# A list scheduler's cost model replaced, and the first loads of a two-layer encoder rearranged

## The chip, the cores and the metric

The kernel runs on one core of one Trainium2 chip. The time is device microseconds (us) of one launch, and the number that counts is the median over runs; before the change it is 1318.05 us (3 runs, 1318.02 to 1319.16).

## The reference

Two layers over 512 tokens of 1024 channels. Each layer modulates a normalised input, projects it, runs three token mixers beside each other, gates and merges them, and adds the result to the input:

```python
c_act = jax.nn.silu(c)
for l in range(DEPTH):
    mod = c_act @ w_ada[l] + b_ada[l]
    shift, scale, gate = jnp.split(mod, 3, axis=-1)
    h = rms_norm(x, norm_w[l]) * (1.0 + scale[:, None, :]) + shift[:, None, :]
    proj = h @ w_in[l]
    ya = mixer_a(...) * silu(ga)   # grouped-query attention, rotary
    yb = mixer_b(...) * silu(gb)   # banded dilated attention, relative bias
    yc = mixer_c(...)              # bidirectional state-space scan, its own gate
    merged = g_a * (ya @ w_proj_a[l]) + g_b * (yb @ w_proj_b[l]) + g_c * (yc @ w_proj_c[l])
    x = x + gate[:, None, :] * (merged @ w_out[l])
```

## The kernel before

Channels lie on partitions and tokens on the free axis. Weights come as chunks of 128x1024 float32 (512 KB; `wch`, 84 a layer). Each is split into a high part (ACT cast, `whi` or `u`) and a low part (a DVE subtraction, `wlo` or `u`), and each product of one 128-channel tile is three matmuls of 128x512: high x high, high x low, low x high (`mm_k`, L490). A whole chunk is 24 of them.

**Modulation.** A load of `w_ada` (128x1024, 512 KB, called an ada here) gives one column of `mod`. `ada` (L637) multiplies it by the broadcast activation `cbc` and sums along the row: on DVE as one instruction with an accumulator, or, for the shifts of tiles 0 to 6 of layer 0 (`POOLADA`, L413), as a GpSimd multiplication (engine POOL) and an ACT pass that sums. Tile i of the normalised input (`norm_tile`, L720) needs the scale `mod[i]` and the shift `mod[8+i]`: DVE makes `tmp`, ACT makes the high part `h`, DVE the low part `h`.

**The start.** `setup` (L534) loads c, the eight tiles of x (`merged<-in_xT`), the vector of small parameters, the identity and the tables of the relative bias, all on SP's queue. `record` (L1307) then goes over the eight tiles: two adas, up to three chunks at a time (`START_W`), the tile, and all matmuls of the `START` chunks (five) that it allows. Each of the five accumulates in a bank of its own. The three bias products (`bias_rows`, L602) come ahead of this.

**The planner.** All instructions are recorded first (`Rec.record`, L199), each with an estimated cost per engine (`cost_pe` to `cost_pool`, L132 to L167) and its predecessors. `Rec.schedule` (L277) is a list scheduler: it keeps an estimated clock, and hands each free engine the ready instruction of the lowest number, if storage can be had. Some instructions may run on one of two or three engines (`either`, L195; `any2`, `scale_p`, `sub`), and go to whichever the plan finds free first. The order found is fixed in the program: each engine works through its list in order. `issue` (L397) emits it, so nearly every instruction in the trace stands at L404.

**Mixer C.** For each of 8 heads and 4 blocks (`ssd_head`, L1162): a diagonal block scaled by a step (`bias<-const,dt`: ACT, POOL or DVE), two scans on DVE (`P<-ps_sc,bias`), an addition (`P<-P`), products with `cb` (`u<-P,u`), a cast on ACT (`u<-u`), the low part (`u<-u`, 128x1024, POOL or DVE), and matmuls into `ps_pv`. The convolution of the next tile (`conv`, L1093: `xs<-tmp,const,xs`, DVE) and fill work for PE (`pump`) lie in between.

Of the kernel before, what the change touches and what calls it, by code (L numbers as in the profile page):

```python
# [36 lines left out]
class V:  # L37
# [68 lines left out]

    def custom(self, fn):
# [16 lines left out]
class Op:  # L124
    __slots__ = ("i", "prio", "alts", "deps", "nd", "succ", "tiles", "frees", "start", "end", "eng", "dma", "ready", "urgent")


LAT = 200
# [3 lines left out]
def cost_pe(name, kw, args):  # L132
    if name == "transpose":
        return max(56, 0.417 * args[1].p * 2 + 2, 0.83 * args[1].n)
    l, r = kw["lhsT"], kw["rhs"]
    if r.dt == F32:
        return 2 * max(0.833 * r.n + 2, 0.833 * l.n, 25)
    return max(0.417 * r.n + 2.5, 0.833 * l.n, 25)


def cost_dve(name, out, ins, ptr, n):
    ps = any(v.t.psum for v in ins) or out.t.psum
    if name == "reciprocal":
        return 69 + 6.25 * n
    if name == "tensor_tensor_scan":
        return 69 + SCAN * n
    if name == "memset":
        return 40 + 0.5 * n
    two = len([v for v in ins if v.n and v.n > 1 and v.n >= n]) > 1
    if not two and not ps and name != "tensor_reduce":  # L150
        return 69 + 0.52 * n + 61 * ptr
    return 69 + 1.042 * n + 61 * ptr


def cost_act(name, out, ins, ptr, acc, n):
    return (52 if ins and ins[0].t.psum else 94) + 0.833 * n + 93 * bool(ptr) + 93 * acc


def cost_pool(name, out, ins, ptr, n):
    if name in ("tensor_scalar",):  # L160
        return 245 + 0.83 * n
    if name == "memset":
        return 100 + 0.4 * n
    return 148 + (2.1 if all(v.n == n and not v.wide for v in ins) else 1.67) * n
# [15 lines left out]
class Rec:  # L180
# [8 lines left out]
    margin = 200  # L189
    wait = 0.4  # L190
# [8 lines left out]
    def record(self, alts):  # L199
# [6 lines left out]
        for eng, meth, args, kw in alts:  # L206
# [11 lines left out]
            if meth == "dma_start":  # L218
                v = out if isinstance(out, V) else reads[0]
                op.dma = v.n * v.p * 4  # L220
                c = 520
            elif eng == "tensor":
                c = cost_pe(meth, kw, args)
            elif eng == "vector":
                if meth == "tensor_reduce":
                    n = reads[0].n
                c = cost_dve(meth, out, reads, ptr, n)
# [6 lines left out]
            op.alts[ENG[eng]] = (c, eng, meth, args, kw)  # L234
        deps = {}
        pe = eng == "tensor"
        for v in reads:
            for o, box, w in v.t.log:
                if w and self.meet(box, v.box):
                    deps[o] = LAT  # L240
        for v in writes:
            if pe and v.t.psum and v.t.lastpe is not None:
                deps.setdefault(v.t.lastpe, 0)
            for o, box, w in v.t.log:
                if o is not op and self.meet(box, v.box) and not (pe and "PE" in o.alts):
                    deps[o] = LAT
# [15 lines left out]
        if op.dma and self.hold is not None:  # L262
            op.alts = {e: (650,) + a[1:] for e, a in op.alts.items()}
# [13 lines left out]
    def schedule(self, reserve):  # L277
# [10 lines left out]
        dma_free, cold = 0.0, 0.0  # L288
        done, now, order = 0, 0.0, []
# [29 lines left out]
        while done < total:  # L319
# [6 lines left out]
            for e in ready:  # L326
                while free[e] <= now and ready[e]:
                    skipped, pick = [], None
                    while ready[e]:
                        it = heapq.heappop(ready[e])  # L330
                        o = it[2]
                        if o.i in started:
                            continue
                        if can_alloc(o, now) and not (soon and waits(o, e)):
                            pick = o
                            break
                        skipped.append(it)
                    for it in skipped:
# [17 lines left out]
                    if e == "PE":  # L356
                        if now - free[e] > 1500:
                            cold = now + 3400
                        if now < cold:
                            c *= 2  # L360
                    o.start, o.eng = now, e
                    free[e] = now + c
                    if o.dma:
                        s = max(now + 1300, dma_free)
                        dma_free = s + max(o.dma / 358.0, 60)
                        o.end = dma_free + 1000
                    else:
                        o.end = now + c
                    order.append(o)
                    done += 1  # L370
                    for z in o.tiles:
                        z.left -= 1
                        z.until = max(z.until, o.end)
                        if z.left == 0:
                            slots[z.tag].append((z.until + LAT, z.slot))
                    for q in o.succ:
                        q.ready = max(q.ready, o.end + q.deps[o] + (self.margin if "PE" in q.alts and e != "PE" else 0))
# [9 lines left out]
            nxt += [f for fr in slots.values() for f, _ in fr if f > now]  # L387
# [1124 lines left out]
```

## Time and profile before

| | us |
|---|---|
| median of 3 runs | 1318.05 |
| profiled execution | 1322.19 |
| its span, first to last instruction | 1320.4 |
| PE (TensorE) busy | 1234.5 |
| DVE (VectorE) busy | 1040.2 |
| ACT (ScalarE) busy | 667.4 |
| POOL (GpSimd) busy | 373.3 |

Busy counts an instruction from its start to its end, so an instruction that is held up within counts as busy for all of that time. A matmul row's length is longer than its share of PE, since matmuls are pipelined: the distance between the starts of two rows, divided by the count, is what one costs. The same goes for DVE.

### The profile page before, as it was taken

To read this page: it belongs to the slowest core of one execution; us is meant where nothing else is said; L and a number is where in the kernel's file an instruction comes from. 1 tells how busy PE (TensorE), PEld (TensorE's weight loads), DVE (VectorE), ACT (ScalarE), POOL (GpSimd) and SP (SyncE) were. 2 spreads that over 40 slices of the span, in tenths; PEclk is the share of its full clock that TensorE was granted. 3 is DMA by queue.
4 is the path that set the end of the run, shared out by engine and by line. 5 is a ranking of instruction groups with operands and counts; after the bars stand their busy time and mean duration, and the time that the engine had idled before them with its cause. 6 is when DMAs were issued, how large, how long until landed. Compare 5 with 4: busy or idle time off the path is not lost.

```text
span 1320.4 us, 17528 instructions
## 1 busy us (share of the span) xinstructions
PE 1234.5 (93%) x6240; PEld 1002.4 (76%) x6240; DVE 1040.2 (79%) x1798; ACT 667.4 (51%) x1132; POOL 373.3 (28%) x322
## 2 busy tenths in 40 slices
PE   4899999989999888999999999999998988989998
PEld 1678888778777667778888788887876866767887
DVE  7979975978799989974675999476598998998642
ACT  4447764666555445333334477556565443543330
POOL 3321220011035759610111222100002268583100
PEclk9999999999999999999999999999999999999999
DMA  7644214545322222234632421253342221222441
GB/s 283 237 122 121 69 47 154 187 140 178 108 59 78 64 64 64 66 110 144 222 129 63 130 96 50 79 183 89 95 132 56 81 64 55 73 64 80 136 137 63
DMA packets 49429, 144.30 MB, mean 109 GB/s; under 512 B 7350, under 2 KB 10038, under 8 KB 49342
## 3 DMA queue, kind: packets, MB, share of 16 engines
q1 hardware_dynamic: 49342, 143.19, 34.9%
q8 instruction: 49, 0.80, 0.3%
q14 instruction: 38, 0.31, 0.1%
HBM read 124.74 MB, written 4.27 MB: 98 GB/s over the span
## 4 chain that ended last, share of the span: by engine, by line
PE 63%; DVE 19%; POOL 7%; ACT 4%; issue 3%; DMA 3%; SPq 1%; DVEq 0%; POOLq 0%; ACTq 0%
PE ps_mm L404 47%; PE ps_sc L404 6%; PE ps_tp L404 6%; PE ps_pv L404 5%; DVE P L404 3%; DVE u L404 3%; POOL u L404 3%; DVE wlo L404 3%; DVE xs L404 2%; POOL P L404 1%; DVE q L404 1%; ACT u L404 1%; POOL bias L404 1%; DVE tmp L404 1%; ACT tmp L404 1%
## 5 line engine op out<-in xcount | busy, mean ns | idle before, releaser
L404 PE MATMUL ps_mm<-h,whi 128*128 128x512 f32 x1840 | 601.4, 397 | 1.8 <-ACT gate L404 1.5
L404 PEld LDWEIGHTS ps_mm<-h,whi 128*128 128x128 f32 x1840 | 345.3, 190 | 77.9 <-ACT gate L404 4.8
L404 PE MATMUL ps_mm<-h,wlo 128*128 128x512 f32 x920 | 364.6, 396 | 0.0
L404 DVE TENSOR_TENSOR wlo<-wraw,whi 128x1024 fp32r<-128x1024 f32 x158 | 208.4, 1321 | 84.6 <-ACT whi L404 83.2
L404 ACT CAST whi<-wraw 128x1024 fp32r<-128x1024 f32 x158 | 165.6, 1049 | 179.6 <-PE ps_mm L404 161.1
L404 PEld LDWEIGHTS ps_mm<-h,wlo 128*128 128x128 f32 x920 | 174.4, 190 | 34.7
L404 PE MATMUL ps_mm<-u,whi 128*128 128x512 f32 (+1 forms) x592 | 172.7, 374 | 0.0
L404 POOL TENSOR_SCALAR P<-P,s 128x512 f32<-128x512 f32 (+1 forms) x63 | 54.9, 873 | 339.3 <-DVE s L404 236.0
L404 PE MATMUL ps_pv<-u,u 128*128 128x256 f32 (+2 forms) x640 | 107.0, 293 | 28.4 <-ACT u L404 15.0
L404 PEld LDWEIGHTS ps_mm<-u,whi 128*128 128x128 f32 x592 | 107.7, 188 | 20.0 <-DVE gate L404 0.6
L404 PEld LDWEIGHTS ps_pv<-u,u 128*128 128x128 f32 (+1 forms) x640 | 81.3, 173 | 48.8 <-ACT u L404 21.2
L404 PE MATMUL ps_mm<-u,wlo 128*128 128x512 f32 (+1 forms) x296 | 110.0, 373 | 0.0
L404 ACT CAST u<-ps_tp 128x512 fp32r<-128x512 f32 (+2 forms) x174 | 71.8, 428 | 57.0 <-PE ps_tp L404 47.6
L404 DVE TENSOR_TENSOR_SCAN P<-ps_sc,bias 128x128 f32<-128x128 f32 (+3 forms) x128 | 98.7, 803 | 0.1
L404 DVE TENSOR_TENSOR u<-ps_tp,u 128x512 fp32r<-128x512 f32 (+2 forms) x174 | 81.9, 487 | 19.6 <-ACT u L404 18.9
L404 PE MATMUL ps_sc<-u,q 128*128 128x256 f32 (+1 forms) x320 | 85.9, 365 | 5.5 <-DMA u<-u 3.5
L404 POOL TENSOR_TENSOR tmp<-tmp,tmp 128x512 fp32r<-128x512 f32 (+1 forms) x22 | 32.4, 1474 | 180.4 <-ACT tmp L404 177.4
L404 POOL TENSOR_TENSOR u<-P,u 128x384 f32<-128x384 f32 (+3 forms) x68 | 69.3, 1030 | 15.0 <-DVE P L404 11.4
L404 PE MATMUL ps_tp<-const,P 128*128 128x128 f32 x448 | 67.6, 273 | 5.6 <-DVE s L404 2.3
L404 PEld LDWEIGHTS ps_tp<-const,P 128*128 128x128 f32 x448 | 53.7, 140 | 19.8 <-issue 7.2
L404 PEld LDWEIGHTS ps_sc<-u,q 128*128 128x128 f32 x320 | 52.9, 191 | 19.8 <-issue 6.5
L404 POOL TENSOR_TENSOR u<-u,u 128x1024 fp32r<-128x1024 f32 x24 | 62.3, 2595 | 12.8 <-ACT u L404 12.8
(163 smaller groups left out, 1892.0 us busy)
## 6 DMA issues: line engine op xcount, KB each, us to landing
wraw<-in_wch SPq DMA_DIRECT2D x168, 512.0 KB, 3.6
wraw<-in_wada SPq DMA_DIRECT2D x32, 512.0 KB, 3.8
u<-u SPq DMA_DIRECT2D x28, 256.0 KB, 3.2
merged<-in_xT SPq DMA_DIRECT2D x16, 256.0 KB, 3.2
whi<-in_wada SPq DMA_DIRECT2D x8, 512.0 KB, 4.9
wlo<-in_wada SPq DMA_DIRECT2D x8, 512.0 KB, 9.0
u<-u SPq DMA_DIRECT2D x64, 64.0 KB, 2.6
tmp<-xs SPq DMA_DIRECT2D x40, 64.0 KB, 2.1
```

Source lines behind the costliest of these rows:

```text
L404: getattr(getattr(nc, eng), meth)(*[get(a) for a in args], **{k: get(v) for k, v in kw.items()})
```

## The change

The planner's numbers are new. Each engine gets a cost and, apart from it, a time to the result (`DVE_TAIL` and the like) in place of one latency of 200; strided views cost more (`apart`); and an instruction that reads two SBUF operands on DVE, or any but memset on POOL, takes a common port, which the plan gives to one of the two at a time. Loads cost more on the queue, and a load between two places in SBUF counts twice its bytes. The planner's reserve for `ps_mm` and its `SOON` change too.

At the start no ada goes to POOL. The shifts of tiles 0, 1 and 2 (adas 8, 9, 10) come in another layout, and PE makes them with eight float32 matmuls of 128x1 each; the other 13 adas go to DVE. The parameters, the identity and a column form of c are loaded from POOL's queue. The bias tables and their products come after the early chunks, and these are six.

```diff
+DVE_TAIL, ACT_TAIL, POOL_TAIL, PE_TAIL = 115, 135, 120, 210
 def cost_dve(...):
-    two = len([v for v in ins if v.n and v.n > 1 and v.n >= n]) > 1
-    if not two and not ps and name != "tensor_reduce":
-        return 69 + 0.52 * n + 61 * ptr
-    return 69 + 1.042 * n + 61 * ptr
+    port = len(sbuf) > 1
...
+    return c, c + DVE_TAIL, port
 def cost_pool(name, out, ins, ptr, n):
-    return 148 + (2.1 if all(v.n == n and not v.wide for v in ins) else 1.67) * n
+        c = 155 + (2.12 if all(v.n == n and not v.wide for v in ins) else 1.67) * n
+    return c, c + POOL_TAIL, True
...
 # Rec.schedule
+                        if o.alts[e][6] and port[other[e]] > now:
+                            skipped.append(it)
+                            if held is None and (len(o.alts) == 1 or port[other[e]] < now + self.patience) \
+                                    and can_alloc(o, now) and not (soon and waits(o, e)):
+                                held = it
+                            continue
...
-                        s = max(now + 1300, dma_free)
-                        dma_free = s + max(o.dma / 358.0, 60)
+                        s = max(now + (1000 if e == "SP" else 1600), dma_free)
+                        dma_free = s + max(o.dma * o.slow / 330.0, 100)
...
-    RESERVE = {..., "ps_mm": 0, ...}
+    RESERVE = {..., "ps_mm": 1, ...}
-    START = ("mm", "mm", "sc", "sc", "pv")
-    POOLADA = (0, 1, 2, 3, 4, 5, 6)
+    START = ("mm", "mm", "sc", "sc", "pv", "pv")
+    POOLADA = ()
+    ADAPE = (8, 9, 10)
-    START_W = 3
+    START_W = (2, 3, 4, 5, 6, 6, 6, 6)
-    SOON = 204
+    SOON = 100
...
 # setup
-        nc.sync.dma_start(self.vec[0], A["vec"][0])
-        nc.sync.dma_start(self.ident, A["ident"])
-        self.bias = self.bias_loads()
+        nc.gpsimd.dma_start(self.vec[0], A["vec"][0])
+        nc.gpsimd.dma_start(self.ident, A["ident"])
+            nc.gpsimd.dma_start(c0, A["ccol"])
...
 # ada
+        if l == 0 and o in self.ADAPE:
+            ps = self.ps("tp", (128, 1))
+            for k in range(8):
+                nc.tensor.matmul(ps, w[:, k * 128:k * 128 + 128], self.ccol[:, k:k + 1], start=(k == 0), stop=(k == 7))
+            nc.vector.scalar_tensor_tensor(self.mod[l][:, o:o + 1], ps, 0.5, self.vec[l][:, V_BADA + o:V_BADA + o + 1],
+                                           op0=ALU.mult, op1=ALU.add)
+            return
...
 # record
-                self.bias_vd = self.bias_rows(*self.bias)
...
+                self.bias_vd = self.bias_rows(*self.bias_loads())
                 self.setup2()
```

What the planner makes of it, at three places. On POOL at the start, from its first memset of 128x512, the order before is this (`wlo` are adas, `const_23` is `cbc`):

```order
L404 MEMSET tmp_479 128x512
L404 ISA
L404 TENSOR_TENSOR wlo_538<-wlo_538,const_23_517 128x1024
L404 TENSOR_TENSOR wlo_562<-wlo_562,const_23_517 128x1024
L404 TENSOR_TENSOR wlo_573<-wlo_573,const_23_517 128x1024
L404 TENSOR_TENSOR wlo_613<-wlo_613,const_23_517 128x1024
L404 TENSOR_TENSOR wlo_666<-wlo_666,const_23_517 128x1024
L404 TENSOR_TENSOR wlo_686<-wlo_686,const_23_517 128x1024
L404 TENSOR_TENSOR wlo_719<-wlo_719,const_23_517 128x1024
```

and the order now, from its first load:

```order
L452 DMA const_1_474<-in_vec 128x116
L452 DMA const_4_480<-in_ident 128x128
L452 DMA s_7_486<-in_ccol 128x8
L452 MEMSET tmp_492 1x128
L452 MEMSET const_11_499 128x1
L452 MEMSET tmp_501 128x512
L452 MEMSET sm_509 1x12
L452 CAST const_128_908<-tmp_868 128x73
L452 CAST const_133_926<-tmp_868 128x16
```

The seven multiplications are gone, and three loads stand ahead of the memsets. On DVE in the same stretch, ahead of the low part of chunk 3 (the last row), the order before is this (`u<-wraw,u` is a chunk's low part, `whi<-whi,const` an ada, `h<-tmp,const,h` a tile's low part, `s` its amplitude):

```order
L404 TENSOR_TENSOR u_74_661<-wraw_555,u_61_625 128x1024
L404 TENSOR_TENSOR const_44_571<-const_44_571,const_19_507 128x1
L404 SCALAR_TENSOR_TENSOR whi_567,const_44_571<-whi_567,const_23_517 128x1024
L404 SCALAR_TENSOR_TENSOR h_673<-tmp_651,const_44_571,h_670 128x512
L404 TENSOR_TENSOR const_44_571<-const_44_571,const_19_507 128x1
L404 SCALAR_TENSOR_TENSOR whi_578,const_44_571<-whi_578,const_23_517 128x1024
L404 SCALAR_TENSOR_TENSOR s_81_690<-const_44_571,const_19_507 128x1
L404 TENSOR_TENSOR const_44_571<-const_44_571,const_19_507 128x1 x2
L404 SCALAR_TENSOR_TENSOR tmp_697<-merged_487,s_81_690,gate_632 128x512
L404 SCALAR_TENSOR_TENSOR s_85_702<-const_44_571,const_19_507 128x1
L404 SCALAR_TENSOR_TENSOR tmp_704<-merged_489,s_85_702,gate_632 128x512
L404 TENSOR_TENSOR u_89_710<-wraw_628,u_84_700 128x1024
```

and now:

```order
L452 SCALAR_TENSOR_TENSOR h_675<-tmp_642,const_42_569,h_668 128x512
L452 TENSOR_TENSOR const_42_569<-const_42_569,const_1_474 128x1
L452 SCALAR_TENSOR_TENSOR s_77_685<-const_42_569,const_1_474 128x1
L452 SCALAR_TENSOR_TENSOR tmp_688<-merged_484,s_77_685,gate_620 128x512
L452 SCALAR_TENSOR_TENSOR whi_576,const_42_569<-whi_576,const_23_523 128x1024
L452 SCALAR_TENSOR_TENSOR wlo_616,const_42_569<-wlo_616,const_23_523 128x1024
L452 SCALAR_TENSOR_TENSOR const_42_569<-ps_tp_681,const_1_474 128x1
L452 TENSOR_TENSOR const_42_569<-const_42_569,const_1_474 128x1 x2
L452 SCALAR_TENSOR_TENSOR s_82_712<-const_42_569,const_1_474 128x1
L452 SCALAR_TENSOR_TENSOR tmp_716<-merged_488,s_82_712,gate_620 128x512
L452 SCALAR_TENSOR_TENSOR h_720<-tmp_688,const_42_569,h_710 128x512
L452 TENSOR_TENSOR u_88_727<-wraw_622,u_85_718 128x1024
```

Two adas of 1024 columns stand in a row where one stood, and a shift is read from PSUM (`ps_tp_681`). In mixer C of layer 0, from the last scan of the fourth head, DVE's order before is this (`xs` is the convolution of the next tiles; the addition `P_5026` and its product are on POOL):

```order
L404 SCALAR_TENSOR_TENSOR P_5026<-ps_sc_4920,bias_4238 128x128
L404 TENSOR_TENSOR tmp_5065<-ps_pv_4940,tmp_5046 64x512
L404 TENSOR_SCALAR xs_5072<-tmp_4975,const_19_507 128x512
L404 TENSOR_SCALAR xs_5077<-tmp_5031,const_19_507 128x512
L404 SCALAR_TENSOR_TENSOR xs_5072<-tmp_4975,const_19_507,xs_5072 128x510
L404 SCALAR_TENSOR_TENSOR xs_5077<-tmp_5031,const_19_507,xs_5077 128x510
L404 SCALAR_TENSOR_TENSOR xs_5072<-tmp_4975,const_19_507,xs_5072 128x511
L404 SCALAR_TENSOR_TENSOR xs_5077<-tmp_5031,const_19_507,xs_5077 128x511
L404 SCALAR_TENSOR_TENSOR xs_5072<-tmp_4975,const_19_507,xs_5072 128x511
```

with this on POOL beside it:

```order
L404 TENSOR_SCALAR bias_4238<-const_21_511,dt_4291 128x128 x2
L404 TENSOR_TENSOR P_5026<-P_5026 128x128
L404 TENSOR_TENSOR u_1052_5033<-P_5026,u_956_4531 128x512
L404 TENSOR_TENSOR u_1065_5098<-u_1052_5033,u_1062_5086 128x1024
L404 TENSOR_TENSOR merged_1198<-merged_1198,gate_5146 128x512
```

and on DVE now, from the same scan:

```order
L452 SCALAR_TENSOR_TENSOR P_5056<-ps_sc_4932,bias_4277 128x128
L452 TENSOR_TENSOR wlo_5080<-wraw_4874,whi_5059 128x1024
L452 TENSOR_TENSOR P_5056<-P_5056 128x128
L452 TENSOR_SCALAR xs_5094<-tmp_5014,const_1_474 128x512
L452 TENSOR_TENSOR u_1056_5050<-P_5056,u_956_4505 128x512
L452 SCALAR_TENSOR_TENSOR xs_5094<-tmp_5014,const_1_474,xs_5094 128x510
L452 TENSOR_SCALAR xs_5107<-tmp_5072,const_1_474 128x512
L452 SCALAR_TENSOR_TENSOR xs_5094<-tmp_5014,const_1_474,xs_5094 128x511
L452 TENSOR_TENSOR u_1070_5117<-u_1056_5050,u_1067_5103 128x1024
L452 TENSOR_TENSOR wlo_5125<-wraw_4985,whi_5114 128x1024
```

The addition, the product and the low part of that head have moved from POOL to DVE, in between the convolution's steps. Over the whole program POOL's list has 218 rows where it had 305.

## Rows read from the trace of the kernel before

**Rows 1.** Page, part 1: busy us (share of the span) xinstructions by engine.
```profile
PE 1234.5 (93%) x6240; PEld 1002.4 (76%) x6240; DVE 1040.2 (79%) x1798; ACT 667.4 (51%) x1132; POOL 373.3 (28%) x322
```

**Rows 2.** Windows: stretch, length, busy us (xcount) by engine, PEclk, DMA share, GB/s.
```profile
20.00:40.00 20.00, 11.92 (x27) 7.27 (x27) 19.82 (x23) 8.83 (x14) 10.61 (x4) 1.00 0.73 286
40.00:60.00 20.00, 15.01 (x56) 11.60 (x57) 19.97 (x35) 8.31 (x14) 8.54 (x5) 0.91 0.60 220
```

**Rows 3.** Timeline of DVE, start; columns: start us, us, instruction [idle before <-releaser].
```profile
13.87 1.23 DVE L404 SCALAR_TENSOR_TENSOR whi<-whi,const 128x1024 f32<-128x1024 f32 x1 [1.28 <-DMA whi<-in_wada]
15.33 2.27 DVE L404 SCALAR_TENSOR_TENSOR s<-const,const 128x1 f32<-128x1 f32 x1
25.05 2.81 DVE L404 SCALAR_TENSOR_TENSOR h<-tmp,const,h 128x512 fp32r<-128x512 f32 x1
...
47.51 1.22 DVE L404 TENSOR_TENSOR u<-wraw,u 128x1024 fp32r<-128x1024 f32 x1
48.65 0.74 DVE L404 SCALAR_TENSOR_TENSOR h<-tmp,const,h 128x512 fp32r<-128x512 f32 x1
49.38 1.21 DVE L404 SCALAR_TENSOR_TENSOR whi<-whi,const 128x1024 f32<-128x1024 f32 x1
...
63.64 0.74 DVE L404 SCALAR_TENSOR_TENSOR h<-tmp,const,h 128x512 fp32r<-128x512 f32 x1
```

**Rows 4.** Timeline of POOL in the same stretch.
```profile
15.25 2.34 POOL L404 TENSOR_TENSOR wlo<-wlo,const 128x1024 f32<-128x1024 f32 x1 [13.69 <-DVE whi L404]
24.23 5.86 POOL L404 TENSOR_TENSOR wlo<-wlo,const 128x1024 f32<-128x1024 f32 x2 [0.20 <-DMA wlo<-in_wada]
```

**Rows 5.** Timeline of PE: start, the early matmuls, and four 128x1 products later on.
```profile
10.66 3.57 PE L404 MATMUL ps_sc<-xs,sm 33*12 33x512 f32 x4 [4.53 <-DMA xs<-in_onehot]
14.16 1.87 PE L404 MATMUL ps_tp<-const,q 128*128 128x1 f32 x8
...
48.78 1.88 PE L404 MATMUL ps_pv<-h,u 128*128 128x512 f32 x4 [1.95 <-DVE u L404]
...
67.49 1.30 PE L404 MATMUL ps_sc<-h,u 128*128 128x512 f32 x5
68.62 0.85 PE L404 MATMUL ps_pv<-h,u 128*128 128x512 f32 x3
69.31 0.60 PE L404 MATMUL ps_tp<-const,tmp 128*128 128x128 f32 x4
...
574.99 0.95 PE L404 MATMUL ps_tp<-const,tmp 128*128 128x1 f32 x8
```

**Rows 6.** Timeline of the loads issued on SP's queue, start.
```profile
1.14 3.68 SPq L404 DMA_DIRECT2D merged<-in_xT  x8
...
9.05 0.35 SPq L404 DMA_DIRECT2D whi<-in_wada  x1
```

**Rows 7.** Waits of PE: us in total, times, longest us.
```profile
PE ps_pv L404 <- ACT u L404: 15.0, 12, 3.9
PE ps_pv L404 <- POOL u L404: 8.8, 8, 2.5
```

**Rows 8.** Timelines of POOL, DVE and PE in mixer C, layer 0.
```profile
468.05 3.96 POOL L404 TENSOR_TENSOR P<-P 128x128 f32<-128x128 f32 x1
...
466.49 0.41 DVE L404 TENSOR_TENSOR_SCAN P<-ps_sc,bias 128x128 f32<-128x128 f32 x1
468.31 3.38 DVE L404 SCALAR_TENSOR_TENSOR xs<-tmp,const,xs 128x510 f32<-128x510 f32 x5
...
474.48 0.50 PE L404 MATMUL ps_pv<-u,u 128*128 128x512 f32 x1 [3.89 <-ACT u L404]
```

**Rows 9.** Windows, from the first scan to the last in mixer C, layer 0.
```profile
406.00:562.00 156.00, 139.81 (x589) 108.28 (x587) 147.79 (x181) 71.80 (x113) 109.46 (x93) 0.99 0.22 66
```

**Rows 10.** Groups, 406 to 562 us: xcount | busy us, mean ns | idle.
```profile
L404 DVE TENSOR_TENSOR wlo<-wraw,whi 128x1024 fp32r<-128x1024 f32 x20 | 31.0, 1552 | 4.4 <-ACT whi L404 4.4
...
L404 POOL TENSOR_TENSOR u<-u,u 128x1024 fp32r<-128x1024 f32 x12 | 31.1, 2594 | 6.4 <-ACT u L404 6.4
```

More of the change, by code (lines that the diff above doesn't have):

```diff
@@ L105, in bitcast, with apart @@
         return r
+    def apart(self):
+        for q in self.path:
+            if q[0] == "rearrange" and q[1][0] == "c (m p) -> c p m":
+                return True
+            if q[0] == "__getitem__":
+                i = q[1][0] if isinstance(q[1][0], tuple) else (q[1][0],)
+                if any(isinstance(x, slice) and x.step not in (None, 1) for x in i):
+                    return True
+        return False
     def custom(self, fn):
@@ L124 @@
 class Op:
[L125 to L128 removed]
+    __slots__ = ("i", "prio", "alts", "deps", "nd", "succ", "tiles", "frees", "start", "end", "eng", "dma", "slow", "ready", "urgent")
+DVE_TAIL, ACT_TAIL, POOL_TAIL, PE_TAIL = 115, 135, 120, 210
 SCAN = 2.083
@@ L155, in cost_act, with cost_dve @@
-def cost_act(name, out, ins, ptr, acc, n):
-    return (52 if ins and ins[0].t.psum else 94) + 0.833 * n + 93 * bool(ptr) + 93 * acc
+        c *= 4 if r.n > 1 else 2
+    return c, c + PE_TAIL
+def cost_dve(name, out, ins, ptr, acc, n):
+    big = [v for v in ins if v.n is None or v.n > 1]
+    sbuf = [v for v in big if not v.t.psum]
+    port = len(sbuf) > 1
+    if name == "memset":
+        c = 40 + 0.5 * n
+    elif name == "reciprocal":
+        c = 69 + 6.25 * n
+    elif name == "tensor_tensor_scan":
+        c = 69 + SCAN * n
+    elif out.apart() or any(v.apart() for v in big):
+        c = 69 + 2.083 * n
+    elif len(big) < 2 and len(sbuf) == len(big) and not out.t.psum and name != "tensor_reduce":
+        c, port = 69 + 0.52 * n + 61 * ptr, n > 1
+    else:
+        c = 69 + 1.042 * n + 61 * ptr
+    c += 75 * acc + 110 * (out.p == 64 and name == "tensor_add")
+    return c, c + DVE_TAIL, port
@@ L159, in cost_pool @@
+def cost_act(name, out, ins, ptr, acc, n):
+    if out.apart() or any(v.apart() for v in ins):
+        c = 94 + 1.9 * n
+    else:
+        c = (52 if ins and ins[0].t.psum else 94) + 0.833 * n + 93 * bool(ptr) + 193 * acc
+    return c, c + ACT_TAIL, False
 def cost_pool(name, out, ins, ptr, n):
-    if name in ("tensor_scalar",):
-        return 245 + 0.83 * n
     if name == "memset":
-        return 100 + 0.4 * n
-    return 148 + (2.1 if all(v.n == n and not v.wide for v in ins) else 1.67) * n
+        c = 100 + 0.85 * n
+        return c, c + POOL_TAIL, False
+    if name in ("tensor_scalar", "tensor_copy"):
+        c = 245 + 0.83 * n
+    else:
+        c = 155 + (2.12 if all(v.n == n and not v.wide for v in ins) else 1.67) * n
+    return c, c + POOL_TAIL, True
@@ L189 @@
     margin = 200
+    patience = 0
     wait = 0.4
@@ L220, in record @@
                 op.dma = v.n * v.p * 4
-                c = 520
+                inside = all(isinstance(z, V) and not z.t.tag.startswith("dram") for z in (out, *reads))
+                op.slow = 2 if inside and reads else 1
+                c = (600 if eng == "sync" else 950, 0, False)
             elif eng == "tensor":
-                c = cost_pe(meth, kw, args)
+                c = cost_pe(meth, kw, args) + (False,)
             elif eng == "vector":
@@ L288, in schedule @@
         dma_free, cold = 0.0, 0.0
+        port = {"DVE": 0.0, "POOL": 0.0}
+        other = {"DVE": "POOL", "POOL": "DVE"}
         done, now, order = 0, 0.0, []
@@ L337, in schedule @@
                         skipped.append(it)
+                    if pick is None and held is not None:
+                        pick = held[2]
+                        skipped.remove(held)
                     for it in skipped:
```

69 lines of the change are left out of this document (38 added, 31 removed).

## The prediction

> **What bounds the kernel now.** I read the page's first part, the windows, the timelines of the start and of mixer C, and the waits of PE. PE is busy 1234.5 of 1320.4 us [rows 1], so 86 us are to be had at most, and an edit counts only by what it takes from them or adds to PE. The waits lie in two kinds of places.
>
> The first is the start. From 20 to 60 us PE works 27 of 40 us while DVE is busy 19.82 and 19.97 of each 20 [rows 2]: DVE sets the pace. But much of that is no work. An instruction of one column takes 2.27 us from 15.33, while a multiplication on POOL runs from 15.25 for 2.34; a tile's low part that takes 0.74 in peace takes 2.81 at 25.05, inside POOL's pair from 24.23 [rows 3, 4]. The two engines shut each other out. PE's last wait of the start ends at 48.78, and it has then a backlog: it runs without a gap until the five early chunks end at 69.31 [rows 5].
>
> The second is mixer C. Matmuls into `ps_pv` wait 15.0 us for ACT's and 8.8 us for POOL's `u` [rows 7]. The longest wait, 3.89 us, begins with an addition of 128 columns on POOL that sits 3.96 us from 468.05 while DVE does five steps of the convolution from 468.31; the product, the cast and the matmuls queue behind it [rows 8]. So here, too, the port is what PE waits for in the end. DVE is busy 147.79 of the 156 us of scans, with such stalls in it [rows 9].
>
> **The start, step by step.** Seven multiplications leave POOL (2.34 us for the one alone) and seven summing passes leave ACT, which was not the bound. Of the sixteen adas DVE had nine; it gets thirteen, PE three. A step of 1024 columns costs DVE 1.14, from one start to the next (47.51 to 48.65); an ada lasts as long (1.21 against 1.22), so I take the same; a step of 512 columns with a small one behind it costs 0.73 (48.65 to 49.38) [rows 3].
> - Before, from the first ada at 13.87 to the end of the last tile's low part at 64.3, 50.4 us: 9 adas, 5 low parts of early chunks and 3 of the next ones (17 x 1.14 = 19.4), 16 steps of 512 (11.7), and some 4 for the inverse root and its wait. That is 35; the other 15 are stalls, two for each multiplication on POOL.
> - Now: 13 adas, 6 + 3 low parts (22 x 1.14 = 25.1), the same 11.7 and 4, and some 1.5 for the shifts that DVE reads from PE: 42.3. The first ada no longer stands behind the bias tables: its load was issued at 9.05, and the x tiles were off SP's queue at 4.8 [rows 6], so the 1.28 us for which DVE waited for it [rows 3] go. From 12.6 that is 54.9, against 64.3.
> - PE then has the last tile of six chunks, 18 matmuls. Eight take 1.82 (67.49 to 69.31), so one is 0.2275 [rows 5], and 18 are 4.1: the end is at 59.0. PE's own sum is close to that: 144 matmuls are 32.8, from about 20 us on, and the first of them are slower. I take 59.5, against 69.3: 9.8 us.
> - The sixth chunk is then done, 24 x 0.2275 = 5.5 us that PE need not do later. The bias products, which ran in PE's waits (3.57 for two of three [rows 5], so 5.4), come where PE is full; for half of that, since the early ones ran slow, I take 2.7 back.
> - The 24 products of 128x1: four took 1.87 at 14.16 and 0.95 at 574.99 [rows 5], so 5.7 to 11.2 us; at the start PE waits anyway. The first seven stand ahead of the transposes that the norm waits for, which I have in the 4 us above, at 1 us.
> - Loads: 22 of 0.52 MB and 2.1 MB of x are 13.6 MB, at 286 GB/s [rows 2] 48 us. The last ada is used at about 51, so this is just hidden; if not, up to 3 us are lost.
>
> Sum of the start: -9.8 - 5.5 + 2.7 = -12.6. Bounds: -18 if PE is as fast from its first matmul as at the end, -4 if DVE is held by loads or shifts.
>
> Three small loads go to POOL's queue, and DVE's first instructions and its `cbc` hang on them. No row shows such a load. Between no delay and one of 3 us I take none: DVE's sums of x wait for the x tiles until about 10 us in any case. The Trainium skill (DMA: Bandwidth & Descriptors, section on the anatomy of one DMA on the gpsimd path) gives some 2 us of fixed cost for a load from this queue, and SBUF — State Buffer (section on the two separate sides) says that DVE in a two-port mode can keep POOL from writing the descriptors. By these, three loads one behind the other would be in at about 7 us, with nothing lost; DVE has no instruction ahead of them that could hold the port. No row here can show it.
>
> **Mixer C.** At the place of the longest wait DVE now does all of it: after the last scan stand a chunk's low part (1.14), the addition (some 0.2 by its 128 columns), one step of the convolution and the product (some 0.5 and 0.7). The addition is over 1.3 us after the scan, where it was over at 472.01, 5.1 after the scan's end at 466.9 [rows 8]; the product, one of 512 columns on either engine, comes at most 0.5 later behind its addition than before. That is 3.3 to 3.8 us less, nearly the whole wait of 3.89. Layer 1 runs the same program, so 7 us for both. Of the 16 us left in the two kinds of wait [rows 7] I take 3 more, since POOL's list shrinks by over a quarter. Against that stands what DVE takes over, by the counts in the order: 8 low parts of 1024 columns, 22 products and 12 additions, 9 sums of the merge, in all some 22 us (9.1 + 8.1 + 2.4 + 2.6, from the same two lengths), nearly all in C, where DVE is the fullest engine. What POOL leaves comes back in stalls: each low part there took 2594 ns, and DVE's chunk subtractions take 1552 ns in this stretch against 1.22 us in peace, 6.6 us for 20 of them alone [rows 10, 3]. For both layers that group gives 13; with the convolution's steps and products 20 to 30. So I set this at +1. Sum for C: -7 - 3 + 1 = -9; bounds -24 (all waits of rows 7) and +22 (no stall goes).
>
> **The rest.** The whole order between is new. PE is nearly full there, and the waits are small and many; I take nothing, with 6 us either way.
>
> **Sum.** -12.6 - 9 = -21.6 us. The profiled execution (1322.2, span 1320.4) would become 1300.6; the median lies 4.1 below it, so 1318.05 becomes 1296.5: I say 1297.
>
> **Rivals.**
> - *DVE overflows in C.* The stalls stay, since the plan's idea of who holds the port drifts from the chip's, and DVE has 22 us more work where it sits at 95%. For: its busy share [rows 9]. Against: at the worst place the work is now on one engine and needs no hand-over. Price: +22, and the waits of PE return at half (+5) with other ones: 1318 - 12.6 + 27 = 1332. It decides as soon as less than 10 us of stalls go.
> - *The start is fed by something else.* Loads, the shifts from PE or PE's slow first matmuls hold it, and C gives nothing: -5 to -7, 1312. For: 48 us of loads against 51. Against: DVE's row of stalls is measured.
> - *The plan fits the chip.* Nearly all of ACT's and POOL's waits in C go, and the rest gains some: -13 more, 1284. For: the waits have one cause. Against: DVE gets no freer.
> - *The change does nothing*: the port isn't the cause. The pairs of rows in [rows 3, 4] leave it little room, and I give it none of its own.
>
> **How the numbers follow.** The forecast (1291 to 1304) gets 0.56, the good plan 0.18, the badly fed start 0.14, the overflow 0.12. Faster here means by over 0.2% (2.6 us), about what can be told from no change. The first two and most of the third are faster: 0.86; same 0.04; slower 0.10. The range, 1282 to 1313, leaves out the overflow and a little at the bottom.
>
> **What would show it.** Right: DVE's small instructions in the first 60 us never over 1 us; the last early tile's low part near 55 us and the early chunks over near 60; no wait over 2 us for `u` at the end of a tile's second head in C; POOL busy near 260. Wrong: DVE idle between 15 and 50 us with a load as the releaser (the second rival); a stretch of scans longer than 158 us with DVE over 95% (the first); or PE waits in the attention stretches that were not there.

## The result, and the profile after

The changed kernel takes 1284.91 us (median of 4 runs, 1284.38 to 1287.1), the kernel before, on the same chip, 1318.61 (1318.02 to 1319.62): a ratio of 0.9747, 95% interval 0.973 to 0.9764, or 33.7 us less. The profiled execution took 1284.8 with a span of 1282.9. The sign and the range hold. The time is not that of the forecast, though (1291 to 1304), but that of the rival with the good plan (1284, chance 0.18). One execution of the run with the early bias tables, below, took 1741.23 us at a mean granted clock of 0.658, where its others show 0.987 or 0.988; nothing here explains it, and it is not counted.

Part 1 of the page after, to be read beside [rows 1]: busy us (share) and instructions by engine.
```profile
PE 1229.2 (96%) x6288; PEld 1009.2 (79%) x6288; DVE 1018.6 (79%) x1876; ACT 668.5 (52%) x1138; POOL 227.2 (18%) x230
```
PE's unused time falls from 85.9 to 53.7 us, so 32 of the 37.5 us of span are PE's waits. POOL has lost 146 us of work and stalls; DVE has 78 instructions more and is busy 22 us less. Read at landmarks of the trace (PE's idle time summed up to there, in brackets):

| us | before | after | difference |
|---|---|---|---|
| early chunks end (five, now six) | 69.1 (22.1) | 63.1 (11.7) | -6.0 |
| first scan, layer 0 | 404.2 (33.0) | 389.2 (21.2) | -15.0 |
| last scan, layer 0 | 560.9 (49.1) | 529.9 (26.7) | -31.0 |
| first scan, layer 1 | 1044.8 (65.4) | 1014.3 (41.0) | -30.5 |
| last scan, layer 1 | 1203.2 (80.6) | 1163.5 (48.3) | -39.7 |
| end of span | 1320.4 (82.5) | 1282.9 (50.2) | -37.5 |

The two stretches of scans give 16.0 and 9.2 us, 25 of the 37.5 (33.7 by the medians; the profiled execution of the kernel before was a long one). Of these 25, PE's idle time is 18.5 (16.1 to 5.5 in layer 0, 15.2 to 7.3 in layer 1); the other 6.7 are PE's busy time, of which the runs don't show how much is work that now stands outside the stretches. The start's idle time falls by 10.4 us, but the products of 128x1, 8.4 us of new work, now stand in that time, so it counts for less than it seems.

Windows after, to be read beside [rows 2, 9]: stretch, length, busy us (xcount) of PE, PEld, DVE, ACT, POOL, granted clock, DMA share, GB/s.
```profile
20.00:40.00 20.00, 18.51 (x79) 15.62 (x80) 17.39 (x36) 6.25 (x8) 0.00 (x0) 1.00 0.87 322
40.00:60.00 20.00, 20.00 (x87) 15.63 (x86) 18.12 (x38) 6.31 (x8) 3.26 (x3) 1.00 0.67 226
389.00:530.00 141.00, 135.47 (x585) 107.16 (x584) 139.67 (x201) 73.46 (x119) 60.81 (x69) 1.00 0.23 71
1014.00:1164.00 150.00, 142.68 (x608) 112.88 (x607) 145.07 (x213) 77.34 (x125) 61.39 (x56) 0.98 0.23 71
```
In layer 0's scans DVE executes 201 instructions in 139.67 us, where it was busy 147.79 in [rows 9] with 181: more work in less time, because the stalls go. (A stall is counted here and below as what an instruction takes beyond 1.15 times the length that a fifth of its kind (same operation, tiles and shape) stay under: 20.8 us there before, 5.7 after; 20.0 and 7.6 in layer 1.) DVE is now busy 139.67 of 141 and PE 135.47: both are nearly full there.

The start of DVE after, to be read beside [rows 3]: start us, us, instruction, [idle before <- releaser].
```profile
4.76 0.44 DVE L452 TENSOR_SCALAR const<-const 128x1 f32<-128x1 f32 x5 [4.76 <-DMA const<-in_vec]
...
12.39 1.22 DVE L452 SCALAR_TENSOR_TENSOR whi<-whi,const 128x1024 f32<-128x1024 f32 x1
...
13.85 0.16 DVE L452 SCALAR_TENSOR_TENSOR s<-const,const 128x1 f32<-128x1 f32 x1
...
32.17 0.16 DVE L452 SCALAR_TENSOR_TENSOR const<-ps_tp,const 128x1 f32<-128x1 f32 x1 [1.93 <-PE ps_tp L452]
...
57.93 0.75 DVE L452 SCALAR_TENSOR_TENSOR h<-tmp,const,h 128x512 fp32r<-128x512 f32 x1 [0.71 <-ACT h L452]
```
The step of one column that took 2.27 us takes 0.16. The first small load on POOL's queue is in at 4.76, and no load ends a wait of DVE after that. What is new are waits for PE: 1.93 us for the third shift. The small loads themselves, first 10 us: KB each, median us from issue to landing (issued at 2.02, 1.27 and 2.56).
```profile
const<-in_ident POOLq DMA_DIRECT2D x1, 64.0 KB, 3.6
const<-in_vec POOLq DMA_DIRECT2D x1, 58.0 KB, 3.5
...
s<-in_ccol POOLq DMA_DIRECT2D x1, 4.0 KB, 4.4
```

PE's start and its products of 128x1, beside [rows 5].
```profile
12.62 1.84 PE L452 MATMUL ps_tp<-const,q 128*128 128x1 f32 x8 [5.51 <-DVE q L452]
14.32 3.12 PE L452 MATMUL ps_tp<-const,wlo 128*128 128x1 f32 x14
...
20.48 1.22 PE L452 MATMUL ps_mm<-h,u 128*128 128x512 f32 x2 [1.86 <-ACT h L452]
21.50 3.41 PE L452 MATMUL ps_tp<-const,wlo 128*128 128x1 f32 x16
...
28.91 0.72 PE L452 MATMUL ps_tp<-const,wlo 128*128 128x1 f32 x6
30.97 1.17 PE L452 MATMUL ps_tp<-const,wlo 128*128 128x1 f32 x10
...
59.11 1.66 PE L452 MATMUL ps_mm<-h,u 128*128 128x512 f32 x6
60.60 1.53 PE L452 MATMUL ps_sc<-h,u 128*128 128x512 f32 x6
61.97 1.52 PE L452 MATMUL ps_pv<-h,u 128*128 128x512 f32 x6
```
The small products before 25 us run at about half the rate of those from 28.91 on (16 records in 3.41 us; 6 in 0.72 and 10 in 1.17). The trace records no granted clock before 28.59 us, so it doesn't say whether the clock is the reason. The 18 matmuls of the last tile take 4.2 us, where 4.1 were worked out.

Waits of PE after, beside [rows 7]: us in total, times, longest.
```profile
PE ps_mm L452 <- DVE merged L452: 15.3, 4, 5.4
...
PE ps_pv L452 <- ACT gate L452: 2.8, 1, 2.8
...
PE ps_pv L452 <- ACT u L452: 1.1, 2, 0.7
```
The two kinds of wait in [rows 7], 23.8 us, are down to 1.1. In their place stands one that was not there: 15.3 us for `merged`. The longest but one of its four, DVE first, then PE:
```profile
372.42 0.68 DVE L452 TENSOR_TENSOR tmp<-tmp,gate 128x512 f32<-128x512 f32 x1
373.14 1.23 DVE L452 TENSOR_TENSOR wlo<-wraw,whi 128x1024 fp32r<-128x1024 f32 x1
374.28 0.69 DVE L452 TENSOR_TENSOR u<-tmp,u 128x512 fp32r<-128x512 f32 x1
...
376.68 1.28 DVE L452 SCALAR_TENSOR_TENSOR merged<-merged,ps_mm 128x512 f32<-128x512 f32 x2
...
371.86 0.39 PE L452 MATMUL ps_mm<-u,wlo 128*128 128x512 f32 x1
377.42 0.79 PE L452 MATMUL ps_mm<-u,whi 128*128 128x512 f32 x1 [5.17 <-DVE merged L452]
...
379.29 4.54 PE L452 MATMUL ps_sc<-u,u 128*128 128x512 f32 x10
```
PE's product is complete at 372.25 and DVE does ten other steps before it reads it. This is an order of steps, not a stall.

### The profile page after: what moved, and what is told of

It reads as the page before. It is cut to its first block, busy times and chain, and to the rows that moved or that the text cites. A ratio compares the mean times of both kernels' runs of the same rounds, so it can differ in the third digit from the quotient of the medians.

```text
span 1282.9 us, 17593 instructions
## 1 busy us (share of the span) xinstructions
PE 1229.2 (96%) x6288; PEld 1009.2 (79%) x6288; DVE 1018.6 (79%) x1876; ACT 668.5 (52%) x1138; POOL 227.2 (18%) x230
## 4 chain that ended last, share of the span: by engine, by line
PE 76%; DVE 11%; DMA 6%; ACT 3%; issue 2%; SPq 1%; POOL 0%; DVEq 0%; ACTq 0%; POOLq 0%
PE ps_mm L452 55%; PE ps_sc L452 8%; PE ps_tp L452 7%; PE ps_pv L452 7%; DVE wlo L452 3%; DMA wraw<-in_wada 2%; DMA u<-u 2%; DVE u L452 2%; DVE xs L452 1%; DVE tmp L452 1%; DVE P L452 1%; ACT whi L452 1%; DVE q L452 1%; DMA wraw<-in_wch 1%; SPq L452 1%
## 5 line engine op out<-in xcount | busy, mean ns | idle before, releaser
L452 PE MATMUL ps_mm<-h,whi 128*128 128x512 f32 x1824 | 593.3, 396 | 4.3 <-ACT gate L452 3.9
L452 PEld LDWEIGHTS ps_mm<-h,whi 128*128 128x128 f32 x1824 | 340.0, 189 | 79.4 <-ACT gate L452 8.6
L452 PE MATMUL ps_mm<-h,wlo 128*128 128x512 f32 x912 | 359.8, 395 | 0.0
L452 DVE TENSOR_TENSOR wlo<-wraw,whi 128x1024 fp32r<-128x1024 f32 x157 | 200.7, 1279 | 71.9 <-ACT whi L452 70.1
L452 PE MATMUL ps_mm<-u,whi 128*128 128x512 f32 (+1 forms) x592 | 177.1, 379 | 16.2 <-DVE merged L452 15.3
L452 DVE TENSOR_TENSOR_SCAN P<-ps_sc,bias 128x512 f32<-128x512 f32 (+3 forms) x128 | 97.6, 803 | 1.6 <-PE ps_sc L452 1.4
L452 PE MATMUL ps_sc<-u,q 128*128 128x256 f32 (+1 forms) x320 | 82.9, 361 | 3.4 <-DMA u<-u 2.7
L452 ACT ACTIVATE bias<-const,dt 128x128 f32<-128x128 f32 x102 | 39.1, 400 | 54.8 <-DVE P L452 50.6
L452 PEld LDWEIGHTS ps_mm<-u,wlo 128*128 128x128 f32 x296 | 56.8, 192 | 9.8
L452 POOL TENSOR_TENSOR tmp<-tmp,tmp 128x512 fp32r<-128x512 f32 (+1 forms) x15 | 20.6, 1375 | 215.1 <-ACT tmp L452 215.1
```

What stands on the lines that cost most here:

```text
L452: getattr(getattr(nc, eng), meth)(*[get(a) for a in args], **{k: get(v) for k, v in kw.items()})
```

## The experiments

Every kernel is planned anew, so an edit moves instructions everywhere. Ratios are against the kernel before in the same session.

**The planner alone.** All edits of the start are undone, the model and the two numbers of the plan stay:
```
-    START = ("mm", "mm", "sc", "sc", "pv", "pv")
-    POOLADA = ()
-    ADAPE = (8, 9, 10)
+    START = ("mm", "mm", "sc", "sc", "pv")
+    POOLADA = (0, 1, 2, 3, 4, 5, 6)
+    ADAPE = ()
...
```


> The new model and the two new numbers of the plan, with the start of before: five early chunks, seven multiplications on GpSimd, bias products early, no products of 128x1, the small loads on SP's queue. Theory (the planner and the start are two separate gains, the planner's lies in mixer C): the scans take about 141 and 149 us as after the change, where they took 157 and 158, the start stays at PE idle 33 us up to the first scan; 1318.6 - 22 = 1297. Rival 1 (the gain in C needs the work that the start has already done): scans over 152 us in both layers, 1308 or more. Rival 2 (the new model also orders the start better, so most of the 34 us is the planner's): 1290 or less.


1291.98 us, ratio 0.9811 (0.9787 to 0.9836). The scans take 140.5 and 149.1 us, as after the whole change, although the start is the old one. The gain in C is the planner's and needs no new start; 25 of the 33.7 us are its own, 5 us more than the 1297 of the theory. The first rival falls; the time lies 2 us above the bound of the second.

**The start alone.** The opposite: the planner, the costs and the numbers of before with the new start.


> The new start alone, with the planner, the costs and the two numbers of before. Theory: PE idles 10 to 12 us less up to the first scan and nothing else changes: 1318.6 - 11 = 1307, scans within 3 us of 157 and 158. Rival 1 (the old plan takes the start's gain away again, since what is ready sooner collides later): 1313 or more. Rival 2 (the start is worth more than it shows in the first 60 us, since six chunks done early free the later stages): 1302 or less.


1311.97 us, ratio 0.9947 (0.9927 to 0.9968): 7 us less, 4 to 10 by the interval. PE's idle time falls by 11.5 us and its busy time rises by 5.3 (1234.5 to 1239.8), so the mechanism is there and the size is little over half of what the prediction gave it (12.6). The scans stay at 156.7 and 159.7. The time lies between the theory (1307) and the first rival (1313).

**The rule of the port taken out.**
```
-            op.alts[ENG[eng]] = (c[0], eng, meth, args, kw, c[1], c[2])
+            op.alts[ENG[eng]] = (c[0], eng, meth, args, kw, c[1], False)
```


> The changed kernel with one thing taken out of the model: the plan no longer keeps VectorE's and GpSimd's instructions that hold the common port from standing side by side. Theory (this rule is what shrank GpSimd's list and with it the stalls and the waits in C): GpSimd is busy over 300 us again, the stalls in C come back to 15 to 20 us a layer, and 15 of the 25 us of C are lost: 1300. Rival (the other costs and the tails of the new model give the gain, the rule is a detail): 1285 to 1290, with GpSimd near 230 us.


1333.18 us, ratio 1.0116 (1.0096 to 1.0137): slower than before by 1.2%. I had expected 1300. (The flag that is taken out stands on more than the text of the change says: also on DVE's steps that read one SBUF operand of more than one column and write to SBUF.) POOL is busy 309.1 us; DVE's additions of 128 columns stall:
```profile
L452 DVE TENSOR_TENSOR P<-P 128x128 f32<-128x128 f32 x33 | 29.0, 887 | 0.1
```
Beside it the same group of the kernel after, with the rule:
```profile
L452 DVE TENSOR_TENSOR P<-P 128x128 f32<-128x128 f32 x30 | 9.5, 318 | 0.0
```
And PE has both the old waits and the new ones:
```profile
PE ps_mm L452 <- DVE merged L452: 14.7, 5, 5.3
PE ps_pv L452 <- ACT u L452: 14.2, 14, 2.4
PE ps_pv L452 <- POOL u L452: 4.0, 6, 1.3
```
The two stretches of scans take 161.6 and 157.8 us, 30 us more than in the kernel after. That is not all of the 51 us between the two traces: 8 are lost ahead of the first scan, 3 between the layers' scans and 10 behind the last. PE idles 28 us more and is busy 22 us more, and its mean granted clock is 0.980 for 0.989.

**The rule alone on the old costs.** The new start and the old model, to which the flag for the port and the wait for it in the plan are added (with `ps_mm` 1 kept back, which the plan needs for storage).


> The kernel with the new start and the old model of costs (old formulas, 200 ns of latency for all, old numbers but one that the plan needs for its storage), to which only the rule of the common port is added. Theory (the rule alone makes the gain in C): GpSimd has near 240 instructions on its list instead of 321, and against the new start with the old planner, 1312, the stalls in C fall from 20 us a layer to under 10: 1288 to 1295. Rival (the rule only works on costs that are close to the chip's, as the new model without the rule was worse than the old one): 1302 or more, with stalls near 15 to 20 us a layer.


1300.31 us, ratio 0.9849 (0.9833 to 0.9866): between the theory and the rival. DVE's additions take 279 ns, POOL is busy 249.7 us, DVE's stalls are 10.5 us in each layer's scans. The waits of [rows 7] are gone here, too, and PE is nearly full in both stretches of scans (first PE's wait, then the stretches, with the columns of the windows above):
```profile
PE ps_pv L444 <- ACT u L444: 3.8, 2, 1.9
...
395.00:547.90 152.90, 148.79 (x641) 118.71 (x640) 147.71 (x201) 79.76 (x131) 75.82 (x69) 0.99 0.25 78
1029.00:1181.50 152.50, 148.39 (x639) 118.43 (x638) 147.68 (x201) 79.72 (x131) 75.81 (x69) 0.99 0.25 78
```
So the rule by itself takes 20 of the 23.8 us of waits, on the old costs. That the stretches are still 152.9 and 152.5 us long is because this plan puts some 640 matmuls into each, where the kernel after has some 580 and 600; the length of a stretch alone doesn't tell how well it runs. With the two runs above this makes a square, all four with the new start:

| us | old costs | new costs |
|---|---|---|
| without the rule | 1312.0 | 1333.2 |
| with the rule | 1300.3 | 1284.9 |

The rule brings 12 us on the old costs and 48 on the new ones; the new costs lose 21 without it and bring 15 with it. Neither is the gain by itself. The square isn't quite clean: `SOON` differs between the columns, and the run at the top left keeps no `ps_mm` back, where the other three keep one. The next run bounds the first of these; the second was not run alone.

**The old number for steps that free PE's results** (`SOON = 204` for 100).


> The changed kernel with the old number for how far the steps that free PE's results are drawn forward (204 for 100). Theory (the number is a detail, the rule of the port and the costs carry the gain): within 4 us of 1284.9 either way, the two long waits for the merged sums (5.17 us at 377 and 5.44 at 656) may move. Rival (the new number is part of the gain): 1290 or more.


1288.51 us, ratio 0.9759 (0.974 to 0.9777), not separable from the kernel after. The waits for `merged` halve (7.0 us in 3), and DVE's stalls in layer 0's scans are 14.3 us for 5.7. A detail that trades one for the other.

**Only the hand-over of the longest wait.** The kernel before, in which one alternative is taken from the planner:
```
-self.any2("tensor_tensor", W[:, n - 128:n], ..., op=ALU.add)
+nc.vector.tensor_tensor(W[:, n - 128:n], ..., op=ALU.add)
```


> The kernel before with one alternative taken from its planner: the addition of 128 columns behind each pair of scans can only go to VectorE (46 of them stood on GpSimd). Theory of the prediction (this hand-over is what the longest wait in C is made of, 3.9 us in each layer, and it goes by itself): the wait of 3.89 us goes and the time falls by 5 to 10 us, 1309 to 1314. Rival (the hand-over is only where the stalls show; VectorE's additions now stall behind GpSimd's instructions instead): 1317 or more, with VectorE's additions far over the 0.28 us that they take in peace.


1334.13 us, ratio 1.0108 (1.0084 to 1.0133). My theory of this step falls, and the rival holds. All 64 additions stand on DVE and take 622 ns each. The place of [rows 8] in this kernel, POOL, then DVE, then PE:
```profile
465.95 2.67 POOL L404 TENSOR_TENSOR u<-u,u 128x1024 fp32r<-128x1024 f32 x1
471.20 6.99 POOL L404 TENSOR_TENSOR u<-u,u 128x1024 fp32r<-128x1024 f32 x1 [2.58 <-ACT u L404]
...
466.29 2.48 DVE L404 TENSOR_TENSOR P<-P 128x128 f32<-128x128 f32 x1
470.80 2.06 DVE L404 SCALAR_TENSOR_TENSOR xs<-tmp,const,xs 128x510 f32<-128x510 f32 x3
473.92 2.06 DVE L404 SCALAR_TENSOR_TENSOR xs<-tmp,const,xs 128x511 f32<-128x511 f32 x3
...
478.24 0.97 PE L404 MATMUL ps_pv<-u,u 128*128 128x512 f32 x3 [4.05 <-POOL u L404]
```
The addition that I wanted on DVE waits there 2.48 us beside POOL's low part, and the next low part of POOL sits 6.99 us (2.4 in the kernel after) beside DVE's convolution. The wait of 3.89 comes back as 4.05 under another name. Moving one of the two partners of a collision moves the collision. (No run takes all of this work off POOL without the rule, so what POOL's shorter list brings apart from the rule isn't shown.)

**Parts of the start, one at a time**, all against the kernel after. Four shifts back on POOL (`POOLADA = (3, 4, 5, 6)`):


> The changed kernel with four of the shifts (3 to 6) multiplied on GpSimd again and summed on ACT; VectorE keeps nine, PE three. Theory (the port sets the start): VectorE saves 4 x 1.14 = 4.6 us of work and gets 4 x 2 = 8 us of stalls, single-column instructions over 1 us return, the early chunks end 3 to 4 us later than 63.1, 1288 to 1289. Rival (PE's slow first matmuls and its 128x1 products set the start): VectorE has slack, the end stays within 1 us of 63.1, 1284 to 1286. Second rival (VectorE's plain amount of work sets it): 2 to 4 us sooner, 1281 to 1283.


1284.81 us, ratio 0.9748 (0.9732 to 0.9763). The place behaves as the theory says: steps of one column take 2.31 and 2.34 us again, and the early chunks end at 68.4. But at the first scan only 1.4 of these 5.3 us are left, and at the end nothing, so the theory's time (1288 to 1289) is wrong.

No shift on PE (`ADAPE = ()`):


> The changed kernel with all sixteen adas on VectorE and none on PE: the 24 products of 128x1 (8.4 us of PE's records) go, and VectorE's waits for them (1.93 us at 32.17 and two small ones), and three adas of 1.14 us come back. Theory, as it stands after the run with four shifts on GpSimd (the start's last microseconds are absorbed by later waits of PE): the early chunks end within 2 us of 63.1 and the time stays within 2 us of 1284.9. Rival 1 (VectorE's work sets the start and that sets the end): 3.4 us later, 1288. Rival 2 (PE's slow small products hold up the start): sooner, 1280 to 1282.


1282.43 us, ratio 0.9717 (0.97 to 0.9733). The last norm step ends at 58.5, against 58.7: without PE's products the start is no sooner, and the early chunks end at 64.3. What DVE no longer waits, it works on the three adas that come back. 2.5 us in favour of leaving the products out, at the edge of what the intervals separate.

Five early chunks for six:


> The changed kernel with five early chunks instead of six. Theory (of the start's gain the sixth chunk is the part that lasts, because its 24 matmuls of 0.2275 us are done while PE would wait and need not be done where it is full): the early chunks end some 3 us sooner, PE's idle time at the start grows, and the whole takes 4 to 5.5 us longer, 1289 to 1290. Rival (this too is absorbed by later waits, as the four shifts were): 1284 to 1286.


1284.98 us, ratio 0.9734 (0.9719 to 0.9748): the theory falls, the rival holds. In the profiled execution PE idles 4.4 us more and is busy 4.0 less, at a mean granted clock of 0.995 against 0.989. The other three executions, at 0.989 to 0.991, take as long, so the clock isn't why the sixth chunk brings nothing.

The bias tables early again:


> The changed kernel with the loads and products of the bias tables at the start again, where they were before. Theory (a part of the start undone alone costs little, since PE's later waits absorb it; the 7 us between the new planner with the old and with the new start come only with several parts together): 1284 to 1287. Rival (this is the part that carries the 7 us, since its loads stand ahead of the adas on SP's queue): 1289 to 1292.


1287.55 us, ratio 0.9761 (0.9742 to 0.978). The interval meets that of the kernel after. So none of the four parts that were undone alone carries the 7 us that the whole start is worth (1291.98 to 1284.91). The small loads on POOL's queue and the order in which the chunks are taken (`START_W`) were not undone alone; which part or pair carries the 7 us is open.

**The new wait taken away.** The two steps of DVE that read PE's results into the merged sums are drawn forward by 300 places:
```
-            self.soon(lambda: nc.vector.scalar_tensor_tensor(g, g, 1.0, p, ...))
+            self.soon(lambda: nc.vector.scalar_tensor_tensor(g, g, 1.0, p, ...), 300)
...
-            nc.vector.scalar_tensor_tensor(x, ps, hg[:, n:n + 1], x, ...)
+            self.soon(lambda: nc.vector.scalar_tensor_tensor(x, ps, hg[:, n:n + 1], x, ...), 300)
```


> The changed kernel in which only the two steps of VectorE that free PE's results into the merged sums are drawn forward by 300 places (the gate's product was drawn by 100, the step with the last projection by none). Theory (the four new waits of PE for merged, 5.17, 5.44, 2.83 and 1.82 us, are a matter of VectorE's order: it has the product on its list and does some eight other steps first): they go, 15.3 us of idle time in four waits shrink to under 5 and the time to 1272 to 1277. Rival 1 (the steps that then come later hold PE up elsewhere): the waits come back under other names, 1281 to 1287. Rival 2 (the clock: PE's granted clock falls after each of the long waits, so more is won than the waits): under 1270.


1285.36 us, ratio 0.9729 (0.9701 to 0.9758). Waits of PE in this kernel:
```profile
PE ps_pv L452 <- ACT u L452: 8.1, 8, 1.9
...
PE ps_sc L452 <- DMA u<-u: 5.8, 5, 3.2
...
PE ps_mm L452 <- DVE merged L452: 1.0, 1, 1.0
```
The wait is gone and 14 us with it, and the time is the same: PE's idle time is 50.3 us again, with the waits for `u` back and DVE's stalls in the scans at 10.3 and 14.5 us for 5.7 and 7.6. The first rival was right.

**The same with other numbers**: merged steps drawn forward by 204 and 200, `SOON` 204, `AHEAD` (how far the loads and casts of chunks are drawn forward) 1400 for 1114, and 4 tiles of `u4` kept back for 5.


> The changed kernel with the merged steps drawn forward by about 200 places, the other steps that free PE's results by 204 again, the chunks' loads and casts by 1400 instead of 1114, and four u4 tiles kept back instead of five. Theory (with the merged waits gone, the plan can give the other numbers more room): 1266 to 1275 and no wait over 3 us after the start. Rival (the numbers are noise on the chip): as the kernel with only the merged steps drawn forward, within 3 us.


1277.63 us (1270.07 to 1280.23), ratio 0.9674 (0.9638 to 0.971), against 0.973 to 0.9764 for the kernel after, which it beats; its interval still meets that of the run before it. PE's idle time is 43.6 us, and after the first 15 us no wait passes 2.9, as the theory says, though the time is over its 1266 to 1275. Which of the four numbers does it isn't told apart.

## Why the prediction was right, and where it was not

**What bounds the kernel** was right: PE's waits are what fell, and both places that I named are where they fell. Of the signs that I gave, two came: no step of one column over 1 us in the first 60 us, and no long wait for `u`. Three came near: 58.7, 63.1 and 227 us where I had 55, 60 and 260.

**The start** (-12.6) was almost twice too large: 7 by the runs. Of its steps, DVE's own sum holds: from 12.39 (12.6 predicted) it is busy 41.6 us for the same list (42.3). What failed is that DVE would not wait: it idles 4.7 us, 2.3 of it for PE's shift products, and the last tile's low part ends at 58.7 in place of 54.9, the chunks at 63.1 in place of 59.5. The products cost 8.4 us, inside the bounds, but "at the start PE waits anyway" doesn't hold for them: those at 21.50, 28.91 and 30.97 stand behind the first early matmul (20.48), and from there to the end of the chunks PE idles only 1.0 us. Nor would it help to leave them out, as the run without them shows (64.3): there PE idles 5.0 us in the same time, for DVE's and ACT's steps. In the new start both engines are nearly full. The second miss is the term "24 matmuls that PE need not do later", 5.5 us: five chunks take as long as six. The third is how I added up: what the early chunks gain is not what the end gains, since PE has waits later on that DVE sets, and these take up what comes to them sooner (5.3 us lost at the chunks were 1.4 at the first scan). The gain shrinks behind the first scan, too: from the planner alone to the whole change the first scan comes 10.9 us sooner (400.1 to 389.2), the end of the span 6.4 (1289.3 to 1282.9). I had treated PE's backlog after the start as unbroken.

**The loads on POOL's queue** cost nothing that the rows show: the first is in at 4.76 us, the third at 2.56 + 4.4 = 7.0. The estimate from the Trainium skill's page (DMA: Bandwidth & Descriptors, section on the anatomy of one DMA on the gpsimd path) gave the same 7 us for the three, but by luck: it took some 2 us for each, one behind the other, where the trace has 3.5 to 4.4 from issue to landing, side by side.

**Mixer C** (-9, bounds -24 and +22) gave 25, just past the bound. The third term, +1 for DVE's added work against the stalls, was near: the steps between the first and the last scan, each at the length that a fifth of its kind stay under, sum to 148 and 151 us where they were 136 and 138 (neighbours overlap a little, so these sums exceed the stretches), and the stalls fell from 41 to 13 us for both layers, 25 against 28. The 22 us that I gave the work was a few too low: the nine sums of the merge, 128x512 each, stand in it at 2.6, and at the 0.73 of my own rows they are 6.6. What failed is the term of the waits. I priced them by the one hand-over that I could see (-7) and gave the other 16 us a fifth. The run with the addition moved shows that the hand-over was not the cause. Nearly all 23.8 us of [rows 7] went together, because they have one cause, two engines planned side by side that can't run side by side: with the rule that keeps them apart these waits are 1.1 us on the new costs and 3.8 on the old ones, without it 18.2 on the new costs (14.2 for ACT's `u` and 4.0 for POOL's). The Trainium skill (SBUF — State Buffer, section on who interferes with whom) says that a DVE instruction with two inputs in SBUF contends with a GpSimd instruction that reads SBUF, and that the order of issue decides which of them blocks. The trace agrees, in both directions: 2.48 us for an addition of 0.28 on DVE, and 6.99 for a low part of 2.4 on POOL.

**The rest** (0, 6 either way) is 1.5 us by the medians: 33.7 less 25.2 for the scans and 7 for the start. But it hides a new loss, the 15.3 us for `merged`. It is close to one of the signs against me ("PE waits in the attention stretches that were not there"), and it came without deciding the result.

**The rivals.** *The plan fits the chip* is what happened in C. Its time was met in part by luck: the start brought 5.6 us less than it counts, and C and the rest 4.7 more. *DVE overflows in C*: DVE is at 99% in layer 0 and 97% in layer 1, as feared, but the stretches are shorter. The run without the rule takes 1333 us, close to the 1332 that I gave this rival, but that is luck: its scans are only 4 us longer than before, where I had put +27 into C, and the rest is lost elsewhere. *The start is fed by something else* is half true: DVE waits for the shifts from PE, not for the loads, but leaving these shifts out brings nothing.

So the chances were rightly signed and the likeliest case was the wrong one of two good ones: -12.6 should have been -7, and -9 should have been -25. The two misses partly cancel, and the range holds by 3 us at its lower end.

## What to carry to other kernels

When several waits in one stretch have a common cause, price them together: either the cause goes and all of them go, or it stays and a repair of the longest only renames it. In a planner, a constraint and the durations that it works on are one change; here the new durations without the constraint were worse than the old ones. And where the bounding engine still waits further on, microseconds won at the start are worth what arrives behind the last of these waits; ask which engine sets that wait before adding them to the sum.

## What the runs showed of the hardware

A long wait of PE was paid for twice here. Windows of the kernel after around the wait of 5.17 us: length, PE busy, granted clock, DMA share, GB/s; below them PE's rows behind the wait.
```profile
356.00:376.00 20.00, 15.63 (x103) 1.00 0.22 58
376.00:381.00 5.00, 3.58 (x8) 0.58 0.22 88
381.00:386.00 5.00, 5.00 (x18) 0.74 0.00 0
386.00:400.00 14.00, 13.87 (x65) 1.00 0.20 46
...
379.29 4.54 PE L452 MATMUL ps_sc<-u,u 128*128 128x512 f32 x10
383.68 0.40 PE L452 MATMUL ps_mm<-u,wlo 128*128 128x512 f32 x1
```
Behind the wait the clock is at its lower level (1.2 GHz, a granted clock of 0.5) for part of two windows. Ten matmuls take 4.39 us there from their start to that of the next row, where ten at the 0.2275 of [rows 5] are 2.3. That is 2.1 us on top of the 5.17 for these ten alone. I had counted waits at their own length. The same fall comes with two of the other three waits for `merged`, those of 5.44 and 2.83 us, and not with the one of 1.82. The last version of the experiments, whose longest wait after the first 15 us is 2.84, shows a mean granted clock of 0.995 to 1.000 in its four executions, against 0.989 to 0.990 in those of the kernel after; how much of its gain that is, the runs don't show.
